# Which engine makes the low parts of the second layer's four key/value weight tiles

## The chip, the core and the metric

The kernel runs on one core of a Trainium2 chip. The metric is the device time of one execution in microseconds (us). The engines are TensorE (PE, matrix products; PEld is its loading of weights), VectorE (DVE), ScalarE (ACT), GpSimd (POOL) and SyncE (SP, which only issues loads here). Each has its own instruction queue and works through it in order; they wait for each other by semaphores.

## The reference, cut to what matters

Two transformer layers run over 512 latent tokens and 256 context tokens of width 1024. Layer 0 is differential attention, layer 1 grouped-query attention with 8 query heads and 2 key/value heads of width 128. What the change touches is the projection to keys and values at the start of layer 1 (`t` is the normalised and modulated stream `h` of the latent tokens, or `hc` of the context):

```python
def project(t):
    p = t @ w_in
    q, k, v, z = jnp.split(p, [GQ_Q_WIDTH, GQ_Q_WIDTH + GQ_KV_WIDTH, GQ_Q_WIDTH + 2 * GQ_KV_WIDTH], axis=-1)
    q = rms_norm(q.reshape(B, L, GQ_HEADS, GQ_HEAD_DIM), qk_g[0])
    k = rms_norm(k.reshape(B, L, GQ_KV_HEADS, GQ_HEAD_DIM), qk_g[1])
```

Keys and values have 256 columns each, for all 768 tokens, and the contraction runs over 1024.

## The kernel before

**Split products.** Every product of the two layers is made of three PE matmuls (`mm3`, L159): each operand is split into a high part, rounded to the matmul's type, and a low part, which is the remainder; high x high, high x low and low x high are summed in PSUM. So each weight tile of 128x1024 passes through `wsplit` (L221): SP loads it into one of two `raw` buffers (L223), ACT writes the high part `whi` (L225), and DVE or POOL writes the low part `wlo` as the difference (L226, by `pieces`, L215). DVE does it in one instruction of 1024 columns, POOL in four of 256:

```python
n = w // -(-w // 256) if eng is nc.gpsimd else w
for i in range(0, w, n):
    eng.tensor_tensor(dst[:, i:i + n], a[:, i:i + n], b[:, i:i + n], op)
```

A raw buffer is free for the next load when both parts are written.

**The stream of tiles.** `WStream` (L237) holds the tiles in the order of their use, and takes the next one as soon as a slot for its two parts is free. Nearly all low parts are DVE's. The exceptions are some of the first tiles of layer 0 and, of the second layer's tiles, those named by `KVE` (L43): tiles 8 to 11 hold the key weights (8 the first half of the contraction, 9 the second) and the value weights (10 and 11 in the same way).

```python
for i in (8, 9, 10, 11):
    ws.add(i, b_w[i], (nc.vector, nc.gpsimd)[KVE[i - 8]])
```

**From layer 0 to layer 1.** The last output product of layer 0 runs over six blocks of 128 tokens (L1365): 0 to 3 are latent, 4 and 5 context. For each block, `resid_a` (L1318) sums squares on ACT (L1292) and multiplies by the gate on DVE (L1322); POOL makes the reciprocal root in two small steps (L421, L422); `resid_b` (L1330) adds the residual on DVE (L1336), ACT sums squares again, POOL adds (L1339, L421), takes the root (L422) and scales the block into `xn` (L1342). Block 5's context rows are loaded by SP into `xn` at L1327. `h1_tr` (L1345) transposes two blocks on PE (L1350), and DVE and ACT make the high and low parts of `h` (L1356 to L1363).

**The key/value stage** follows a written order, `KV` (L44): `k`, `v` are the 24 matmuls of one token block against the key or the value weights (`proj_tok`, L1270: eight contraction steps of three matmuls; steps 0 to 3 read the first tile of the pair, 4 to 7 the second, and each step reads one 256-column piece of it), `t` is one `h1_tr` of the context blocks 4 and 5, and `c` transposes finished keys. The order begins k0, k1, v0, k2, t0, k3. The tiles 8 to 11 are released together at L1458.

**What sets the order of instructions.** The program is written in a certain order, with priorities (`high_priority`, `hot`). A scheduler then simulates it and lets each engine take, each time that it is free, the ready instruction of the highest priority; that order is fixed in the program that runs.

Of the kernel before, what the change touches and what calls it, by code (L numbers as in the profile page):

```python
# [39 lines left out]
PRE = 16.26  # L40
TS = 9.04
HFD = 2
KVE = (0, 1, 0, 1)  # L43
KV = (('k', 0), ('k', 1), ('v', 0), ('k', 2), ('t', 0), ('k', 3), ('c', 0), ('v', 1), ('v', 2), ('t', 1), ('k', 4), ('c', 1), ('c', 2), ('k', 5), ('v', 3), ('v', 4), ('c', 3), ('c', 4), ('v', 5), ('c', 5))  # L44
SPL = 3.06
GAP0 = 6.86
# [41 lines left out]
def tile_backbone(  # L88
# [213 lines left out]
    for i in (8, 9, 10, 11):  # L302
        ws.add(i, b_w[i], (nc.vector, nc.gpsimd)[KVE[i - 8]])
    for kind, i in [("q", 0)] + fill1:
# [1511 lines left out]
```

## Time and profile before

| | us |
|---|---|
| median of three runs | 792.78 (792.57 to 792.84) |
| the profiled execution | 792.77 |
| its span in the profile | 790.8 |
| busy: PE, DVE, ACT, POOL | 776.8, 522.4, 455.4, 324.9 |
| TensorE's granted clock, share of full speed | 0.999 |

The span runs from the first to the last instruction; the 1.97 us between it and the execution's time lie around it. PE is busy for 98% of the span, so an engine that is not PE counts where PE waits for it. The stretch that the change touches is from about 510 to 545 us of the span. In the rows below, an instruction has its start, its length, its engine, its line, its operation, what it writes and reads, and in brackets the idle time of its engine just before it and what ended that. L155 is the line of the helper that issues the matmuls.

### The profile page before, as it was taken

Reading aid. Unit: us, or ns where it says so; the run is one execution under the profiler, and the core shown is the slowest. Engines: PE = TensorE matmul, PEld = TensorE weight load, DVE = VectorE, ACT = ScalarE, POOL = GpSimd, SP = SyncE. Lnnn points to the kernel's source line nnn. Section 1 sums busy time; section 2 is a strip of 40 time slices with the busy share of each in tenths; the row PEclk is TensorE's granted clock in tenths of the full one; section 3 lists DMA queues with packets and bytes.
Section 4 is the critical chain, followed back from the end, with each engine's and each line's share of the span. In section 5 each row is a group of like instructions: output and inputs, shape, how many; then the busy total and the mean of one; then the engine's idle time right before and its main releaser. Section 6 shows DMA issues by size and latency. Waiting matters only on the chain.

```text
span 790.8 us, 14236 instructions
## 1 busy us (share of the span) xinstructions
PE 776.8 (98%) x5446; PEld 699.2 (88%) x5446; DVE 522.4 (66%) x940; ACT 455.4 (58%) x994; POOL 324.9 (41%) x434
## 2 busy tenths in 40 slices
PE   8999999999999999999999999999999999999996
PEld 6688888988887898888979998899999999989986
DVE  4666677786769637866578753567558977565634
ACT  5546546675575644775468843565456676676632
POOL 1121375663338542353425411585446654234101
PEclk9999999999999999999999999999999999999999
DMA  9934211131422322323330151041423512010102
GB/s 339 384 97 148 80 54 59 50 104 67 138 80 83 118 81 68 120 80 107 117 97 31 51 213 54 1 140 53 159 82 101 153 43 81 27 54 28 54 27 107
DMA packets 35092, 77.77 MB, mean 98 GB/s; under 512 B 3408, under 2 KB 10064, under 8 KB 35024
## 3 DMA queue, kind: packets, MB, share of 16 engines
q1 hardware_dynamic: 31168, 71.05, 26.9%
q10 hardware_dynamic: 3856, 5.81, 2.1%
q8 instruction: 43, 0.70, 0.3%
q14 instruction: 25, 0.20, 0.1%
HBM read 70.56 MB, written 2.10 MB: 92 GB/s over the span
## 4 chain that ended last, share of the span: by engine, by line
PE 89%; DVE 3%; ACT 3%; DMA 2%; POOL 1%; issue 1%; SPq 0%; DVEq 0%; ACTq 0%; POOLq 0%
PE bk L155 56%; PE sc L155 10%; PE bk L167 9%; PE sc L994 5%; PE bk L1059 3%; PE bk L1558 3%; PE bk L835 1%; DMA xnt<-in_xlT 1%; PE sc L1023 1%; POOL wlo L219 1%; DMA raw<-in_b_w 1%; DVE al L1063 1%; PE bk L406 1%; PE bk L407 1%; ACT p L1033 0%
## 5 line engine op out<-in xcount | busy, mean ns | idle before, releaser
L155 PE MATMUL bk<-whi,h 128*128 128x256 f32 (+1 forms) x1184 | 243.7, 299 | 0.0
L155 PE MATMUL bk<-h,whi 128*128 128x512 f32 (+2 forms) x864 | 227.9, 347 | 0.0
L155 PEld LDWEIGHTS bk<-whi,h 128*128 128x128 f32 x1184 | 191.8, 191 | 10.5 <-issue 4.0
L155 PE MATMUL bk<-wlo,h 128*128 128x256 f32 (+1 forms) x592 | 175.7, 299 | 0.0
L155 PEld LDWEIGHTS bk<-h,whi 128*128 128x128 f32 x864 | 149.9, 189 | 17.1 <-issue 2.9
L155 PE MATMUL bk<-h,wlo 128*128 128x512 f32 (+2 forms) x432 | 149.6, 346 | 0.0
L233 POOL TENSOR_SCALAR p<-p,sm 128x768 f32<-128x768 f32 (+1 forms) x80 | 71.7, 899 | 163.1 <-DVE sm L1005 63.9
L155 PEld LDWEIGHTS bk<-wlo,h 128*128 128x128 f32 x592 | 112.6, 191 | 3.8 <-issue 0.7
L219 DVE TENSOR_TENSOR wlo<-raw,whi 128x1024 fp32r<-128x1024 f32 (+1 forms) x66 | 80.7, 1226 | 34.4 <-ACT whi L225 34.3
L155 PEld LDWEIGHTS bk<-h,wlo 128*128 128x128 f32 x432 | 81.5, 189 | 7.1 <-issue 0.2
L225 ACT CAST whi<-raw 128x1024 fp32r<-128x1024 f32 x64 | 67.2, 1050 | 32.9 <-PE bk L155 27.8
L1002 ACT ACTIVATE p<-sc,sm 128x768 f32<-128x768 f32 (+1 forms) x68 | 59.5, 878 | 30.6 <-DVE sm L999 30.1
L999 DVE TENSOR_REDUCE sm<-sc 128x1 f32<-128x768 f32 (+1 forms) x68 | 60.3, 917 | 19.2 <-PE sc L994 19.2
L219 POOL TENSOR_TENSOR sz<-sz,za 128x192 f32<-128x192 f32 (+1 forms) x48 | 35.1, 752 | 65.8 <-ACT za L199 65.7
L1010 DVE SCALAR_TENSOR_TENSOR p<-p,sm,p 128x768 f32<-128x768 f32 (+1 forms) x34 | 40.3, 1186 | 7.4 <-POOL p L233 5.1
L994 PE MATMUL sc<-qk,qk 64*128 64x384 f32 (+1 forms) x396 | 43.8, 351 | 0.7 <-ACT p L1002 0.7
L1562 DVE TENSOR_TENSOR al<-bk,ah 128x512 fp32r<-128x512 f32 x48 | 32.1, 686 | 18.4 <-ACT ah L1561 18.2
L1062 ACT CAST ah<-bk 128x512 fp32r<-128x512 f32 x56 | 31.6, 589 | 19.0 <-PE bk L1059 16.6
L1063 DVE TENSOR_TENSOR al<-bk,ah 128x512 fp32r<-128x512 f32 x56 | 37.4, 683 | 6.7 <-ACT ah L1062 6.5
L1543 ACT ACTIVATE p<-sc,sm,qrs 128x768 f32<-128x768 f32 x32 | 31.9, 996 | 15.1 <-DVE sm L1540 8.9
L994 PEld LDWEIGHTS sc<-qk,qk 64*128 64x128 f32 x396 | 32.8, 184 | 7.7 <-issue 3.4
L1561 ACT CAST ah<-bk 128x512 fp32r<-128x512 f32 x48 | 26.9, 588 | 17.9 <-PE bk L1558 14.6
(240 smaller groups left out, 1492.6 us busy)
## 6 DMA issues: line engine op xcount, KB each, us to landing
raw<-in_a_w SPq DMA_DIRECT2D x28, 512.0 KB, 3.5
araw<-in_ada_w SPq DMA_DIRECT2D x12, 1024.0 KB, 5.2
raw<-in_b_w SPq DMA_DIRECT2D x20, 512.0 KB, 3.5
ag<-in_ada SPq DMA_DIRECT2D x16, 512.0 KB, 7.9
raw<-in_w_out SPq DMA_DIRECT2D x16, 512.0 KB, 3.5
sw<-qr ACTq DMA_DIRECT2D x32, 128.0 KB, 2.1
gw<-in_ada_w SPq DMA_DIRECT2D x8, 512.0 KB, 4.1
xnt<-in_xlT SPq DMA_DIRECT2D x4, 512.0 KB, 5.6
```

Source lines behind the costliest of these rows:

```text
L155: i = nc.tensor.matmul(o, a, b, start=start, stop=stop)
L167: nc.tensor.matmul(o, v[:, kt + e, c], a[:, e * 256:e * 256 + 256], start=first and i == 0, stop=last and i == 5)
L219: eng.tensor_tensor(dst[:, i:i + n], a[:, i:i + n], b[:, i:i + n], op)
L225: nc.scalar.copy(hi, r)
L233: (nc.vector if eng == "v" else nc.gpsimd).tensor_scalar(dst, src, s_, 1.0, ALU.mult, ALU.mult)
L994: prev = nc.tensor.matmul(sc[m][:, j if nk == T else m, :w], a[r, tok], b[r, c], start=i == 0, stop=i == 2)
L999: nc.vector.tensor_reduce(mx, scv, AX.XY if nk == T else AX.X, ALU.max, negate=True)
L1002: nc.scalar.activation(pv_, scv, AF.Exp, bias=mx, accum_out=l[:, m:m + 1])
L1010: nc.vector.scalar_tensor_tensor(ps_[0], pt, r, ps_[0], ALU.mult, ALU.add)
L1063: nc.vector.tensor_tensor(al, tr, f32(ah), ALU.subtract)
L1543: nc.scalar.activation(pt.rearrange("p (j n) -> p j n", j=2), scv, AF.Exp, scale=sr, bias=nmx, accum_out=l)
L1562: nc.vector.tensor_tensor(al, tr, f32(ah), ALU.subtract)
```

## The change

The four entries of `KVE` are turned round: POOL makes the low parts of tiles 8 and 10, DVE those of tiles 9 and 11. Before, DVE makes 8 and 10, and POOL 9 and 11. Loads, high parts, products and the written order stay as they are.

```diff
 HFD = 2
-KVE = (0, 1, 0, 1)
+KVE = (1, 0, 1, 0)
```

## Rows read from the trace of the kernel before

**Rows 1.** The page: span, and PE's busy time, share and instructions.

```profile
span 790.8 us, 14236 instructions
...
PE 776.8 (98%) x5446; PEld 699.2 (88%) x5446; DVE 522.4 (66%) x940; ACT 455.4 (58%) x994; POOL 324.9 (41%) x434
```

**Rows 2.** Windows: length, busy PE, PEld, DVE, ACT, POOL, clock, DMA share, GB/s.

```profile
517.00:530.00 13.00, 12.63 (x107) 12.43 (x105) 8.31 (x11) 9.23 (x27) 10.67 (x16) 1.00 0.59 199
530.00:556.00 26.00, 25.65 (x216) 25.65 (x217) 17.10 (x44) 12.80 (x38) 14.08 (x20) 1.00 0.14 42
556.00:576.00 20.00, 20.00 (x170) 20.00 (x169) 10.41 (x25) 8.67 (x30) 10.35 (x18) 1.00 0.45 159
...
700.00:760.00 60.00, 59.56 (x402) 55.19 (x401) 34.39 (x60) 35.66 (x71) 16.21 (x20) 1.00 0.11 36
```

**Rows 3.** Waits of PE, 440 to 791 us: total, times, longest.

```profile
PE sc L1350 <- POOL xn L1342: 0.7, 1, 0.7
PE sc L155 <- ACT p L1543: 0.4, 1, 0.4
```

**Rows 4.** Timeline of PE: the first key matmuls, and around 530 us.

```profile
517.00 0.48 PE L155 MATMUL bk<-whi,h 128*128 128x256 f32 x2
517.32 0.28 PE L155 MATMUL bk<-wlo,h 128*128 128x256 f32 x1
...
529.36 0.28 PE L155 MATMUL bk<-whi,h 128*128 128x256 f32 x1
530.35 1.09 PE L1350 MATMUL sc<-ident,xn 128*128 128x128 f32 x8 [0.72 <-POOL xn L1342]
```

**Rows 5.** Chain that ended last, 500 to 545 us: start, length, what.

```profile
518.49 4.74 DMA raw<-in_b_w
...
523.26 1.06 ACT whi L225
...
527.93 0.49 POOL sm L421
...
529.17 1.13 POOL xn L1342
```

**Rows 6.** Timeline of POOL, 514 to 527 us.

```profile
514.37 0.89 POOL L1339 TENSOR_SCALAR sm<-sm 128x1 f32<-128x1 f32 x1 [2.38 <-ACT jk L1292]
515.34 3.13 POOL L219 TENSOR_TENSOR wlo<-raw,whi 128x256 fp32r<-128x256 f32 x4
518.42 0.34 POOL L421 TENSOR_TENSOR sm<-sm 128x1 f32<-128x1 f32 x2
...
524.39 2.83 POOL L219 TENSOR_TENSOR wlo<-raw,whi 128x256 fp32r<-128x256 f32 x4 [1.98 <-ACT whi L225]
```

**Rows 7.** Timeline of DVE, 512 to 523 us.

```profile
512.03 1.42 DVE L1336 SCALAR_TENSOR_TENSOR gate<-u,sm,gate 128x512 f32<-128x512 f32 x2 [0.53 <-POOL sm L422]
...
513.96 1.22 DVE L219 TENSOR_TENSOR wlo<-raw,whi 128x1024 fp32r<-128x1024 f32 x1
...
521.31 1.63 DVE L1336 SCALAR_TENSOR_TENSOR xn<-u,sm,xn 128x512 f32<-128x512 f32 x1 [0.45 <-POOL sm L422]
```

**Rows 8.** Timeline of ACT, 512 to 526 us.

```profile
512.09 1.06 ACT L225 CAST whi<-raw 128x1024 fp32r<-128x1024 f32 x1
...
514.18 1.04 ACT L225 CAST whi<-raw 128x1024 fp32r<-128x1024 f32 x1
...
525.36 0.18 ACT L1292 ACTIVATION_READ_ACCUMULATOR jk<-xn 128x1 f32 x1
```

**Rows 9.** Timeline of SP's queue of loads, 515 to 517 us.

```profile
515.21 0.33 SPq L223 DMA_DIRECT2D raw<-in_b_w  x1
516.87 0.33 SPq L1327 DMA_DIRECT2D xn<-in_xc  x1
```

**Rows 10.** The page's DMA issues: count, KB each, median us to landing.

```profile
raw<-in_b_w SPq DMA_DIRECT2D x20, 512.0 KB, 3.5
```

**Rows 11.** POOL's line 1339, 440 to 530 us: least, median, greatest ns.

```profile
L1339 POOL TENSOR_SCALAR sm<-sm x6: 213/224/887, 492.5 to 527.3; 128x1 f32<-128x1 f32 x6
```

## The prediction

> **What bounds the kernel now.** I read the page first: TensorE (PE) is busy for 776.8 of 790.8 us [rows 1], so time can only be won or lost where PE idles. The table of windows [rows 2] shows where: from 556 to 576 us it is busy throughout, in 517 to 530 it lacks 0.37 us, in 530 to 556 another 0.35, in 700 to 760 another 0.44. The waits of PE over the whole second layer [rows 3] name only two: 0.7 us for GpSimd's (POOL's) `xn`, and 0.4 us for an exponential, far from the change. PE's timeline gives the first its place [rows 4]: the last matmul before it starts at 529.36, the next work, the eight transposes of normalised row block 5, only at 530.35. Matmuls of 256 columns follow each other at 0.12 us (three in the 0.36 us of one contraction step), so PE was free at 529.48 and starts 0.87 us late; the trace counts 0.72 of it as idle, and I use 0.72.
>
> The chain of waits [rows 5] and POOL's timeline [rows 6] then say why. All four key/value weight tiles pass through here. Tile 11's low part holds POOL from 524.39 to 527.22, ahead of the three small steps and the scaling that make `xn`; that scaling starts at 529.17 and releases PE at 530.35. So one of the two low parts that POOL makes now stands in the chain that PE waits for. It is the fourth tile's, and that one goes to VectorE (DVE).
>
> **The change part by part.** Work in all: DVE makes two low parts at 1.22 us each [rows 7] before and after, POOL two of four pieces at 2.83 and 3.13 us [rows 6]. Nothing is added; cost 0. What moves is which tile waits for which queue.
>
> Tile 11 leaves POOL. POOL's four pieces (2.83 us) no longer stand at 524.39. The sums that L1339 and L421 read come from ScalarE (ACT), whose square sums of block 5 follow tile 11's cast (it ends at 523.26 + 1.06 = 524.32 [rows 5]) by two passes, the second of which is read out by 525.36 + 0.18 = 525.5 [rows 8]. Today L421 starts at 527.93 and `xn` ends at 530.30, 2.37 us later [rows 5]. From 525.5 it would end at about 527.9, 1.6 us before PE is free at 529.48. So the 0.72 goes, and with 1.6 us in hand. DVE takes tile 11 in its place: 1.22 us, beside PE. What is late next is nothing that the waits of PE show until 700 us.
>
> Tile 10 comes to POOL. Its load needs a raw buffer, which is freed now by DVE's tile 8 at 515.18 (the issue is at 515.21 [rows 9]). After the change the first of the two buffers is free when DVE has made tile 9 or POOL tile 8, both at about 516.3 to 516.5 (next paragraphs): 1.2 us later. A load takes 3.5 us in the median and the slowest here 4.74 [rows 5, 10], the cast 1.06, the four pieces 2.83 to 3.13. So tile 10's low part is done between 516.4 + 3.5 + 1.06 + 2.83 = 523.8 and 516.4 + 4.74 + 1.06 + 3.13 = 525.3. That is early enough for POOL to start on `xn` at 525.5. PE comes to the first value product at 517.00 + 2 x 8 x 0.36 = 522.8 and wants the pieces from 522.9 on: between nothing and 1.3 us of waiting. I take 0, by the row that it is nearest to: tile 11's low part is late today by far more (due at 522.8 + 4 x 0.36 = 524.2, complete at 527.22) and PE has no idle before 529.5 [rows 2, 4, 6], since the order that the scheduler writes puts the third key product and transposes in between. 1.3 stays as the upper end.
>
> SP's queue: tile 10's load moves back from 515.21 to about 516.4, next to the context rows' load at 516.87 [rows 9], which is also on block 5's path; tile 11's load, at 518.49 now [rows 5], can go at about 517. Three loads of 512 KB then start within 0.7 us rather than 3.3. If each takes as long as the slowest of today, the context rows land 0.6 us later (516.87 + 4.74 = 521.6, against the DVE step that uses them at 521.31 [rows 7]). That is inside the 1.6 us in hand; cost 0, upper end 0.6 off the same cover.
>
> Tile 8 comes to POOL. Its cast starts at 512.09 and takes 1.06 [rows 8], so its input is there at 513.15. POOL is idle for 2.38 us before 514.37, waiting for ACT [rows 6]. The four pieces can run from 513.2 to 516.3 (3.13 us, the longer of the two sets); PE first reads a low part at 517.32 [rows 4] and one more piece every 0.36 us. Cost 0, with 1 us in hand. Behind the pieces stands L1339 of block 4, now at 514.37 and then at about 516.4; but its followers L421 come only at 518.42 today, behind tile 9's pieces [rows 6], and those pieces are gone, so block 4 is no later. The other end of this cost is 2.4 us; it is the second rival.
>
> Tile 9 goes to DVE. The cast ends at 514.18 + 1.04 = 515.2 [rows 8], DVE lost tile 8's 1.22 us at 513.96, so the part is ready by about 516.5; PE wants it at 517.32 + 4 x 0.36 = 518.8. POOL makes it by 518.47 today. Cost 0, and more in hand than now.
>
> **Sum.** The profiled execution took 792.77 us (span 790.8 and 1.97 around it), and the median of the runs is 792.78, so the two stand for each other. 792.77 - 0.72 = 792.05; I say **792.1 us**, a gain of 0.09%. About 0.2% (1.6 us) is what a measurement of this kernel can tell from no change, so this counts as the same.
>
> **Where rows speak against it.** DVE's instructions with two inputs in on-chip memory hold POOL up: L1339 on POOL takes 224 ns in the median of six and 887 once [rows 11], that once from 514.37 to 515.26, and DVE's tile 8 ends at 515.18 [rows 6, 7]. It goes the other way too: DVE's step at 521.31 took 1.63 us where the two steps of the block before took 1.42 together [rows 7]. The Trainium skill ("GPSIMD Engine Reference", section Key points) says that GpSimd shares its SBUF interfaces with VectorE and contends with instructions of two SBUF inputs; the trace agrees. The same page (section Engine selection) would give element-wise work to VectorE, GpSimd being about twice as slow with two inputs; here it is 3.13 against 1.22, and by that rule the tile that PE needs first should not go to POOL. What this would do is worked out in the second rival.
>
> **Rivals.**
> 1. *The wait stays.* Block 5 is held by something other than tile 11: its context rows land late because three loads now run together, or tile 10's pieces sit in front of L1339. For it: tile 10's worst case ends at 525.3, the loads' at 521.6, and if both slip by another microsecond or two the 1.6 in hand are gone. Against: that needs two worst cases at once. Time: 792.8, within 0.4. Chance 0.24.
> 2. *PE waits for tile 8's low part at 517.3: slower.* If the order puts POOL's L1339 first, as it stands now, the pieces run from 515.34 for 3.13 us to 518.47; DVE's tile 9 (1.22 us from about 515.8) now falls into that stretch and holds them up to 519.7. PE wants the first piece at 517.32. If it waits for the whole tile it stands for 2.4 us; the 0.72 at 530 is still won, so 792.77 + 2.4 - 0.7 = **794.5** (+0.2%). If PE waits piece by piece, the first is there at some 517.3 and next to nothing is lost. It decides from the moment that the last piece ends later than 517.32 + 0.72 = 518.0. For it: the hold-up is in the trace. Against: POOL's idle stretch lies open before 514.37, and where tile 9's and tile 11's casts came just ahead of ACT's sums, the order put all four pieces ahead of the small steps [rows 6]. Chance 0.15, half of it beyond +0.2%.
> 3. *The order downstream changes.* The order on every engine comes from a simulated schedule, and one that runs from 517 us on differently may fall out differently to the end. To gain, there is only the idle of 0.37 + 0.35 + 0.44 = 1.16 us up to 760 [rows 2], so 791.6 at best, and perhaps half a microsecond of stalls that modelled ends of matmuls hide: 791.1. To lose, there is more room: two more waits like the one at 530 make 793.5, five of them 795.6. Against: PE is so full from 543 to 576 that the order should settle again. Chance 0.13: 0.05 faster, 0.06 slower, the rest between.
>
> That the swap does not happen is no case: the engine is named in the call, and nothing else decides it.
>
> **How the numbers follow.** Forecast 0.48 (791.6 to 792.5), rivals 0.24, 0.15 and 0.13. Beyond 0.2% slower than 792.78, over 794.4: half of rival 2 and half of rival 3, 0.14 in all. Beyond 0.2% faster, under 791.2: 0.05, from rival 3 alone. The rest, 0.81, is the same. The range from 791.1 to 794.5 holds forecast, rival 1, the bound of rival 2 and the gain of rival 3; it leaves out mainly the long losses of rival 3 and mishaps that come together.
>
> **What would show it.** In the changed kernel's trace: POOL makes low parts from about 513.2 and again between 521 and 525, none after; DVE makes one near 515.5 and one near 525; L1339 to `xn` of block 5 ends near 528; PE's wait for `xn` is gone from its list and the 517 to 530 window is full. Wrong, if PE waits for a low part at 517 or 523, if its wait for `xn` is still there, or if the windows after 543 differ by more than a few tenths of a microsecond; then the order downstream has changed and the cause lies there.

## The result and the profile after

The changed kernel takes **794.88 us** in the median of ten runs (794.22 to 797.15), the kernel before, beside it on the same chip, 792.69 (792.39 to 793.29). The ratio is 1.0029, with a 95% interval from 1.0021 to 1.0038: 2.2 us slower, just outside the range that was given, and on the other side of no change. The changed kernel's profiled execution took 797.15 us (span 795.2), the longest of its ten; the others lie between 794.22 and 795.64. So its trace holds some 2 us that a usual run does not have. An estimate below puts 1.7 of them on TensorE's clock; there is no trace of a usual run, so the sizes are taken from timed experiments.

The page of the changed kernel, the lines that answer to [rows 1]:

```profile
span 795.2 us, 14236 instructions
...
PE 778.6 (98%) x5446; PEld 699.9 (88%) x5446; DVE 526.5 (66%) x940; ACT 456.0 (57%) x994; POOL 324.7 (41%) x434
```

Its table of windows, columns as in [rows 2]:

```profile
517.00:530.00 13.00, 12.71 (x105) 12.24 (x104) 9.73 (x13) 9.21 (x24) 10.18 (x15) 1.00 0.54 182
530.00:543.00 13.00, 10.79 (x77) 10.31 (x76) 9.14 (x28) 5.50 (x19) 6.81 (x12) 0.87 0.09 32
543.00:556.00 13.00, 13.00 (x112) 13.00 (x110) 8.83 (x15) 5.93 (x17) 6.87 (x8) 1.00 0.20 60
556.00:576.00 20.00, 20.00 (x170) 20.00 (x169) 10.27 (x22) 9.13 (x29) 6.84 (x13) 1.00 0.42 147
```

The instructions are the same in number. The loss is in one window: from 530 to 543 us PE lacks 2.21 us (before, 0.35 from 530 to 556) and issues 77 matmuls, where the full window behind it has 112. A further part is the clock: the granted share is 0.87 there, and 0.57 from 534 to 538, so PE ran for a while at the lower of its two levels (1.2 instead of 2.4 GHz), right behind its longest wait. An estimate of what that cost, from the row: (1 - 0.87) x 13 = 1.7 us. PE's timeline marks the stage: from the first key product to the first transpose of queries it is 56.24 us before (517.00 to 573.24) and 60.29 after (517.35 to 577.64); from there to the last matmul it is 211.25 in both. Nothing changes behind the key/value stage.

The waits of PE from 440 to 796 us of the changed kernel, as [rows 3]:

```profile
PE bk L155 <- DVE kn L1430: 1.6, 1, 1.6
PE sc L1350 <- POOL xn L1342: 0.6, 1, 0.6
PE sc L155 <- ACT p L1543: 0.4, 1, 0.4
PE bk L155 <- POOL wlo L219: 0.2, 1, 0.2
```

PE's timeline at the two long ones, as [rows 4]:

```profile
531.38 1.09 PE L1350 MATMUL sc<-ident,xn 128*128 128x128 f32 x8 [0.60 <-POOL xn L1342]
534.09 0.55 PE L155 MATMUL bk<-whi,h 128*128 128x256 f32 x1 [1.61 <-DVE kn L1430]
```

The chain that ended last, from 500 to 550 us, as [rows 5]:

```profile
518.80 4.46 DMA raw<-in_b_w
...
523.29 1.06 ACT whi L225
...
525.57 2.37 DVE xn L1336 x2
...
527.97 5.33 DMA gq<-in_b_qk_g
...
533.42 0.62 DVE kn L1430 x2
```

The wait for `xn` that the change was to remove (0.7 in [rows 3]) is still there with 0.6, and a longer one stands behind it: for the normalised keys `kn`, whose gains `gq` (L1383) are loaded late. (The bracket of `kn` in DVE's rows below names POOL's L1410; the chain has the load of `gq`, which landed at 533.30, and where that load comes early, in gq_early below, the wait for `kn` is 0.2.) The chain names the way there, and three timelines show its links. SP's queue of loads, as [rows 9]:

```profile
518.37 0.80 SPq L223 DMA_DIRECT2D raw<-in_b_w  x2
519.23 0.42 SPq L1327 DMA_DIRECT2D xn<-in_xc  x1
```

POOL, as [rows 6]:

```profile
513.57 4.78 POOL L219 TENSOR_TENSOR wlo<-raw,whi 128x256 fp32r<-128x256 f32 x4 [1.24 <-ACT whi L225]
518.43 0.22 POOL L1339 TENSOR_SCALAR sm<-sm 128x1 f32<-128x1 f32 x1
...
523.12 4.25 POOL L219 TENSOR_TENSOR wlo<-raw,whi 128x256 fp32r<-128x256 f32 x4 [1.34 <-ACT whi L225]
527.63 0.38 POOL L1339 TENSOR_SCALAR sm<-sm 128x1 f32<-128x1 f32 x1 [0.25 <-ACT jk L1292]
...
530.20 1.12 POOL L1342 TENSOR_SCALAR xn<-xn,sm 128x1024 f32<-128x1024 f32 x1
```

DVE, as [rows 7]:

```profile
513.70 2.38 DVE L1363 TENSOR_TENSOR h<-hf,h 128x512 fp32r<-128x512 f32 x2
515.99 1.76 DVE L219 TENSOR_TENSOR wlo<-raw,whi 128x1024 fp32r<-128x1024 f32 x1
...
524.37 1.27 DVE L219 TENSOR_TENSOR wlo<-raw,whi 128x1024 fp32r<-128x1024 f32 x1 [1.29 <-ACT whi L225]
525.57 2.36 DVE L1336 SCALAR_TENSOR_TENSOR xn<-u,sm,xn 128x512 f32<-128x512 f32 x2
527.85 1.28 DVE L1363 TENSOR_TENSOR h<-hf,h 128x512 fp32r<-128x512 f32 x2
533.42 0.61 DVE L1430 SCALAR_TENSOR_TENSOR kn<-bk,qrs,gq 128x128 f32<-128x128 f32 x2 [4.29 <-POOL qrs L1410]
```

POOL's low part of tile 8 takes 4.78 us, not 3.13, with DVE's L1363 and tile 9 beside it, which are slowed too (2.38 against 1.28 for the same pair at 527.85; 1.76 against 1.27). It ends at 518.35, and SP's load of tile 10, which takes over its buffer, is issued at 518.37; before it was 515.21 [rows 9]. The order on SP's queue has changed as well: both value tiles stand ahead of the context rows, which go from 516.87 to 519.23. Three loads now start within 0.9 us. What came early before is late on every queue behind it. The context rows land at 524.60, 3.6 us later than before (521.02). Tile 11's low part stands on DVE ahead of block 5's residual (L1336), which starts at 525.57 instead of 521.31 [rows 7]. Where a residual waits for nothing but its rows, it starts 0.1 us behind their landing (dve_all below), so of these 4.3 us tile 11 holds some 0.9, and the late rows the rest. POOL's pieces of tile 10 stand ahead of L1339 (523.12 to 527.37), but L1339 then waits another 0.25 us for ACT, so they are not what holds it. ACT's queue issues `gq` only at 527.97, behind block 5's square sums (before: 523.65), to land 5.33 us later.

### The profile page after: what moved, and what is told of

Same layout as the page of the kernel before. It is cut to its first block, busy times and chain, and to the rows that moved or that the text cites. A ratio compares the mean times of both kernels' runs of the same rounds, so it can differ in the third digit from the quotient of the medians.

```text
span 795.2 us, 14236 instructions
## 1 busy us (share of the span) xinstructions
PE 778.6 (98%) x5446; PEld 699.9 (88%) x5446; DVE 526.5 (66%) x940; ACT 456.0 (57%) x994; POOL 324.7 (41%) x434
## 4 chain that ended last, share of the span: by engine, by line
PE 87%; DVE 4%; ACT 3%; DMA 3%; issue 1%; POOL 1%; SPq 0%; DVEq 0%; ACTq 0%
PE bk L155 55%; PE sc L155 10%; PE bk L167 8%; PE sc L994 5%; PE bk L1558 3%; PE bk L1059 2%; PE bk L835 1%; DMA xnt<-in_xlT 1%; DMA sw<-qr 1%; DMA gq<-in_b_qk_g 1%; ACT whi L225 1%; DVE al L1063 1%; DMA raw<-in_b_w 1%; PE sc L1023 1%; POOL wlo L219 1%
## 5 line engine op out<-in xcount | busy, mean ns | idle before, releaser
L1062 ACT CAST ah<-bk 128x512 fp32r<-128x512 f32 x56 | 31.6, 589 | 19.0 <-PE bk L1059 16.6
L1059 PE MATMUL bk<-ident,p 128*128 128x128 f32 x224 | 35.2, 276 | 2.0 <-DVE gate L1133 1.1
```

Source lines behind the costliest of these rows:

```text
L1059: nc.tensor.transpose(tr[:, e * 256 + i * P:e * 256 + (i + 1) * P], a[:, j * P:(j + 1) * P], ident)
```

## The experiments

In the table "over before" is the ratio with its 95% interval, against runs of the kernel before on the same chip; an interval reaches 0.7 to 1.0 us to either side. "Stage" is the time on PE's timeline of the one profiled execution from the first key product to the first transpose of queries.

| run | median us | over before | stage us |
|---|---|---|---|
| before | 792.5 to 792.8 | | 56.24 |
| after | 794.88 | 1.0029 [1.0021, 1.0038] | 60.29 |
| after_again | 794.83 | 1.0027 [1.0017, 1.0038] | 60.24 |
| keys_only | 794.40 | 1.0021 [1.0012, 1.0030] | 57.85 |
| values_only | 795.31 | 1.0029 [1.0017, 1.0040] | 58.67 |
| gq_early | 794.11 | 1.0019 [1.0010, 1.0028] | 57.40 |
| after_late11 | 793.47 | 1.0012 [1.0004, 1.0021] | 56.80 |
| gq_late11 | 793.26 | 1.0008 [0.9999, 1.0016] | 56.61 |
| gq_xc | 795.59 | 1.0037 [1.0025, 1.0050] | 58.80 |
| gq_xc_late11 | 794.98 | 1.0029 [1.0017, 1.0041] | 58.37 |
| after_own | 798.32 | 1.0073 [1.0060, 1.0085] | 61.84 |
| own_ordered | 794.13 | 1.0020 [1.0011, 1.0029] | 57.64 |
| before_own | 793.94 | 1.0018 [1.0009, 1.0027] | 58.10 |
| before_xn_first | 794.27 | 1.0021 [1.0012, 1.0030] | 57.70 |
| pool_9_only | 793.25 | 1.0007 [0.9998, 1.0016] | 56.86 |
| dve_all | 793.46 | 1.0011 [1.0003, 1.0020] | 57.84 |

**after_again: the changed kernel once more.** No edit.

> The changed kernel once more, unaltered, because the execution that was profiled (797.15 us) is the slowest of its ten (median 794.88). Theory A (block 5 is late: SP's queue has the loads of tiles 10 and 11, held up by POOL's tile 8, ahead of block 5's context rows; from there PE waits for the key norm's gains gq, whose load stands on ACT's queue behind block 5's square sum, and for xn): median 794.2 to 795.6, and the two waits of PE are there again at about 530 to 534 us, the one behind gq shorter than 1.6 us or without the drop of the granted clock after it. Theory B (the order further down has changed, and the waits at 530 are chance): the two waits are much smaller, and PE loses its time after 543 us.

794.83 us, and the same trace: waits of 1.5 us for `kn` and 0.6 for `xn`. Its profiled execution (796.69) is again the longest, so the two profiles are the two longest of 17 runs. The slowdown is real; the 1.5 to 1.6 us at `kn`, and the clock of 0.87 from 530 to 543 us in both, are what these two executions show.

**keys_only and values_only: half of the change each.**

keys_only:

```diff
-KVE = (1, 0, 1, 0)
+KVE = (1, 0, 0, 1)
```

> Half of the change: POOL makes the low part of tile 8 and DVE that of tile 9; tiles 10 (DVE) and 11 (POOL) as in the kernel before. SP's order has tiles 10 and 11 ahead of block 5's context rows, as in the changed kernel. Theory A, by which tile 8 on POOL and SP's order are the cause: 794.2 to 795.6, as slow as the whole change. A rival, by which the value tiles are the cause (tile 10's four pieces on POOL, tile 11 on DVE ahead of block 5's residual): 792.2 to 793.2.

values_only:

```diff
-KVE = (1, 0, 1, 0)
+KVE = (0, 1, 1, 0)
```

> The other half: POOL makes the low part of tile 10 and DVE that of tile 11; tiles 8 (DVE) and 9 (POOL) as before. SP's order has block 5's context rows between the two loads, as in the kernel before. Theory A: no loss, and the gain that the prediction saw in tile 11's leaving POOL: 791.9 to 792.7, PE's wait for xn gone. The rival, by which the value tiles are the cause: 794 to 795.5.

keys_only, with POOL on tiles 8 and 11, costs most of the loss by itself and meets its first expectation: again 4.78 us for tile 8, again both value loads ahead of the context rows (518.02 and 518.87), and PE waits 1.1 us for `xn`. POOL's pieces of tile 11 take 4.16 us there, with block 5's later residual beside them, and hold L1339 until 528.30 (before: 2.83 us, until 527.22). values_only keeps the loads as before and does take the wait for `xn` away, as the prediction's step said; but it is no faster, as PE waits elsewhere: 0.54 us for `kn` at 531.59, 0.31 at 556.57 and 0.92 for `vl` at 558.29. Its first expectation was wrong. Its time lies in the rival's range, but not for the reason given there: tile 11 stands behind block 5's residual on DVE (525.60; the residual runs from 521.53 to 523.43). The wait for `vl` comes behind the low part of a later weight tile (on DVE from 556.69 to 557.90), so the order has changed further down the stage. A loss as large as the whole change's thus comes here with the loads on time and the residual first. The halves don't add up: 1.6 and 2.6 us alone, 2.1 together.

**gq_early, after_late11, gq_late11: the two late placements undone, one by one and together.** gq_early issues the gains' load early on ACT's queue, into a buffer that is free then; after_late11 has DVE make tile 11's low part behind block 5's residual; gq_late11 does both.

```diff
-    xn = {}
+    xn, early = {}, last_of(nc.scalar)
...
-        gq = t1p.tile([P, 2, P], F32, name="gq")
-        nc.scalar.dma_start(gq, b_qk_g.partition_broadcast(P))
+        gq = con.tile([P, 2, P], F32, name="gq")
+        with tc.issue_after(early): nc.scalar.dma_start(gq, b_qk_g.partition_broadcast(P))
```

```diff
...
-        pieces(eng, lo, r, f32(hi), ALU.subtract)
+        with tc.issue_after(mark[0]) if key == 11 else nullcontext(): pieces(eng, lo, r, f32(hi), ALU.subtract)
...
-    ws.release(*wout_keys(0, c, n))
+    mark.append(last_of(nc.vector)); ws.release(*wout_keys(0, c, n))
```

> The changed kernel with one load moved: the key norm's gains gq get memory of their own and are loaded before layer 0's last product ends, so that nothing waits for them; the order on PE, DVE, POOL and SP stays as it is, and on ACT only this load moves. Theory A: PE's wait behind gq (1.6 us in the profile, with some 1.7 us at the lower clock after it) goes, xn's 0.6 stays: 792.8 to 793.6, that is 1.3 to 2.1 us under the changed kernel. Theory B: no change, 794.5 to 795.3.

> gq_early with DVE's low part of tile 11 put behind block 5's residual; SP's order stays. Theory A1: the residual waits for its rows, which land at 524.4, so it starts 0.7 earlier than in gq_early and the time falls by 0.3 to 0.7 at most, 793.4 to 793.8. Theory A2: 0.7 to 1.0 less, 793.1 to 793.4, with PE's wait for xn gone.

> The changed kernel with one order undone: DVE's low part of tile 11 is issued behind block 5's residual instead of ahead of it; the key-norm gains' load stays where it is, on ACT's queue behind block 5's square sums. Theory A (that one placement is the head of the later waits: residual, square sum, gains' load and key norm all stand behind it): the residual starts near 524.0 instead of 525.6, the gains' load is issued near 526.4 and has landed by 531.7, PE's waits for xn and kn are 0.5 or less each; 793.0 to 793.7. Theory B (it takes both edits, the gains' load is a loss of its own): the wait for kn stays at 1 us or more, 794.0 to 795.0.

Over the kernel before on its own chip, the changed kernel stands at +2.07 us (after_again), gq_early at +1.35, after_late11 at +0.95, gq_late11 at +0.62. So the gains' load is worth 0.7 alone, outside both expectations and between them, and tile 11's place on DVE 1.1; together they give back 1.45 of the 2.07, less than their sum. The trace of after_late11 fits that: with the residual earlier, `gq` goes out at 526.55 by itself. These are rough sizes. The single runs of gq_early and the changed kernel overlap; nine of after_late11's eleven runs stand less over their before than any of the changed kernel's 17, and it meets its first expectation in time, in the residual's start and in both waits. In gq_early and in after_late11 the granted clock is full again throughout the window in which it had fallen; gq_early's row:

```profile
530.00:543.00 13.00, 12.19 (x102) 11.72 (x101) 11.35 (x31) 6.40 (x20) 9.13 (x13) 1.00 0.02 6
```

What is left of PE's waits in after_late11 is tile 11 itself, which that expectation did not have:

```profile
PE bk L155 <- DVE wlo L219: 0.7, 1, 0.7
PE sc L155 <- ACT p L1543: 0.4, 1, 0.4
PE bk L155 <- DVE kn L1430: 0.2, 1, 0.2
```

No wait for `xn` is left. Its DVE timeline has the residual ahead of tile 11 and 1.4 us earlier than in the changed kernel, 0.1 us behind the landing of its rows (524.06):

```profile
524.16 2.35 DVE L1336 SCALAR_TENSOR_TENSOR xn<-u,sm,xn 128x512 f32<-128x512 f32 x2 [1.53 <-POOL wlo L219]
526.43 1.21 DVE L219 TENSOR_TENSOR wlo<-raw,whi 128x1024 fp32r<-128x1024 f32 x1
```

DVE makes the tile in one instruction, so no piece of it is there before 527.64, and PE waits until 527.70; on POOL, before, the first of four pieces was done at 525.13. So on DVE tile 11 costs in either place: ahead of the residual by what stands behind it, behind the residual by itself.

**gq_xc and gq_xc_late11: the context rows on another queue.** Both have gq_early's edit; block 5's rows are loaded from ACT's queue, so that they need not stand behind the value tiles on SP's; the second has the late tile 11 too.

```diff
-            nc.sync.dma_start(t, xc[(m - NQ) * P:(m - NQ + 1) * P, :])
+            (nc.sync if m == NQ else nc.scalar).dma_start(t, xc[(m - NQ) * P:(m - NQ + 1) * P, :])
```

> gq_early (794.11 us) with block 5's context rows loaded from ACT's queue instead of SP's, so that they no longer stand behind the loads of tiles 10 and 11; DVE and POOL keep their order. Theory A1 (SP's queue is what makes block 5 late): DVE's residual of block 5 starts near 522 instead of 525.1, PE's 0.6 for xn and 0.2 for the key norm go: 793.0 to 793.4. Theory A2 (DVE's own order is what holds it: tile 11's low part, which waits for its late load, stands ahead of the residual): the residual still starts when tile 11 is done, about 525, and the time stays within 0.2 of 794.1.

> gq_early with both: the context rows from ACT's queue and tile 11's low part behind the residual. Either theory: the residual starts near 522, POOL's pieces of tile 10 are what is left ahead of xn, PE's waits for xn and the key norm go, and only the wait for tile 10's pieces (0.8 us in gq_early) is left: 792.8 to 793.3. If it stays at 794, block 5 is held by POOL's tile 10 and not by SP or DVE.

Both missed in time, and both are slower than their twins without this edit, by 1.6 and 1.7 us (each over its own before). The rows go out at 517.0. In gq_xc the residual still starts behind tile 11 on DVE, as theory A2 has it, but at 526.69, since tile 11 is later too. In gq_xc_late11 it starts at 522.73, and L1339 then stands behind tile 10's pieces on POOL until 528.88. But now tile 10's load starts 1.1 us behind a load already under way, and its high part begins at 523.08 and 523.53 instead of 521.55 (after_late11): PE waits 0.6 and 1.1 us for `whi` and 0.8 and 0.7 for tile 10's pieces. Loads of 512 KB that are under way together land one behind the other: at 521.98, 523.26 and 524.60 in the changed kernel, at 520.58, 523.05 and 524.44 in gq_xc. Putting one first made another the late one, so these runs have no early rows without a late tile 10.

**after_own, own_ordered, before_own: the loads of tiles 10 and 11 don't wait for POOL.** Tiles 10 and 11 get two buffers of their own. own_ordered also sets two orders by hand: tile 10's pieces behind block 4's scaling, tile 11's low part behind block 5's residual.

```diff
-        r = wp.tile([P, 1024], F32, tag="raw", name=nm("raw"), bufs=2)
+        r = (rawp[0] if key in (10, 11) else wp).tile([P, 1024], F32, tag="raw", name=nm("raw"), bufs=2)
...
-    u0, ss = {}, {}
+    u0, ss = {}, {}; rawp.append(bp)
```

> The changed kernel, but the loads of tiles 10 and 11 get two buffers of their own, so neither waits until POOL has written tile 8's low part. Theory A (the loss comes from that wait: tile 8's low part, held up to 4.8 us beside DVE's instructions, frees its buffer only at 518.3, and three loads then start together): the two loads are issued well before 517, tile 8's low part still takes over 4 us on POOL, POOL's scaling of block 5 no longer has tile 10's pieces in front of it, PE's wait for xn falls under 0.2 and those for kn and low parts go; from the first key product to the first query transpose 56.4 us or less (60.2 in the changed kernel, 56.2 before), time 791.9 to 793.0. Rival B (the loss is the sharing of POOL and DVE itself, or the order of the stage, not the buffer): at least 58 us for the stage and 794.0 to 795.5.

> The kernel before with the same two buffers for tiles 10 and 11. Its tile 10 already loads from 515.2 on; tile 11, now from 518.5 on, can come earlier. Theory A (what PE waits for at 530 is tile 11's low part in POOL's queue, as its load comes late): xn is done before PE asks for it, that wait (0.7 us) goes and the time is 791.9 to 792.4. Rival B (the order changes and gives it back elsewhere, as with values_only and pool_9_only): 792.6 to 794.0.

> The changed kernel with buffers of their own for tiles 10 and 11 (as in after_own) and two orders set by hand: POOL makes tile 10's low part behind block 4's scaling, DVE tile 11's behind block 5's residual. Theory A (what after_own lost comes from the order that the scheduler wrote, not from the early loads): stage of 56.8 us or less, 792.3 to 793.4, no wait of PE over 1 us. Rival B (two low parts on POOL with DVE's instructions beside them are too slow for the stage wherever they stand): tile 10's pieces again take over 4 us, PE waits 1 us or more for h, kn or xn, 794.5 to 798.

Here a theory fell: that the time comes back when tiles 10 and 11 are loaded early. They are (from 462.66 and 463.67 on in after_own), and after_own is the slowest of all. But the runs do not take the whole delay away. The weight tiles behind them in SP's order now wait for the buffers of tiles 8 and 9, and block 5's context rows still stand behind these two loads (after_own):

```profile
518.00 0.80 SPq L223 DMA_DIRECT2D raw<-in_b_w  x2
518.90 0.38 SPq L1327 DMA_DIRECT2D xn<-in_xc  x1
```

The rows land at 524.13, and in own_ordered at 523.89, about as late as in after_late11 (524.06). So what the late rows cost is not measured by these runs. The timeline of POOL in after_own has tile 8 unchanged and tile 10 early, as meant:

```profile
513.17 4.81 POOL L219 TENSOR_TENSOR wlo<-raw,whi 128x256 fp32r<-128x256 f32 x4 [1.23 <-ACT whi L225]
...
519.17 4.43 POOL L219 TENSOR_TENSOR wlo<-raw,whi 128x256 fp32r<-128x256 f32 x4
523.59 1.12 POOL L1342 TENSOR_SCALAR gate<-gate,sm 128x1024 f32<-128x1024 f32 x1
```

But that tile 10 now stands ahead of block 4's scaling, 3.9 us later than in the changed kernel (519.71), and the order of the stage behind it differs: PE waits 2.4 us for an `h` at 542.56, and the granted clock is 0.89 from 543 to 556. The time lies beyond both expectations. own_ordered, with the loads still early, wins 4.2 of the 5.8 us back, yet ends at 794.13: its tile 10 (520.15 to 523.85 on POOL) stands ahead of block 5's first reciprocal root, so the residual starts at 524.68, no earlier than in after_late11. Its time is between both expectations. Early loads of tiles 10 and 11 alone bring nothing here; early rows with them were not tried. before_own (+1.4 us) missed its first expectation and lies in its rival's range: PE's wait for `xn` falls to 0.4, and one of 0.7 for `kn` comes in.

**before_xn_first, pool_9_only, dve_all: the gain that was predicted, tried in other ways.** before_xn_first leaves every tile on its engine and has POOL make tile 11's pieces behind block 5's scaling; pool_9_only and dve_all give POOL only tile 9, or none. before_xn_first:

```diff
-        pieces(eng, lo, r, f32(hi), ALU.subtract)
+        with tc.issue_after(mark[key]) if key in mark else nullcontext(): pieces(eng, lo, r, f32(hi), ALU.subtract)
...
-    ws.release(*wout_keys(0, c, n))
+    mark[11] = last_of(nc.gpsimd); ws.release(*wout_keys(0, c, n))
```

> The kernel before, with POOL's low part of tile 11 issued behind block 5's scaling instead of ahead of it. Theory A (the step of the prediction called Tile 11 leaves POOL, without moving any tile to another engine): xn ends near 527.9 instead of 530.3, PE's wait for it goes, 791.9 to 792.4. Rival B (PE then comes to tile 11's low part before POOL has made it, about 531): a wait for wlo of 0.5 to 2 us takes its place, 793 to 794.5.

pool_9_only:

```diff
-KVE = (0, 1, 0, 1)
+KVE = (0, 1, 0, 0)
```

> POOL makes only tile 9's low part, DVE those of 8, 10 and 11: the one step of the prediction that was to bring the gain (tile 11 leaves POOL), without tiles 8 and 10 coming to it. If that step was right by itself: PE's wait for xn gone, nothing else late, 791.9 to 792.5. Rival: DVE with three tiles is late with the residual or with the key norm, and PE waits there: 793 to 795.

dve_all:

```diff
-KVE = (0, 1, 0, 1)
+KVE = (0, 0, 0, 0)
```

> DVE makes all four low parts, POOL none; raw buffers as before. Theory A (low parts on POOL are what holds buffers and xn up; DVE makes one in 1.2 us and has room): loads of tiles 10 and 11 are issued by 517, no xn wait, 791.9 to 793.0. Rival B (DVE becomes the engine that the stage waits for: two more low parts of 1.2 us stand in front of block 5's residual and of the high-low splits that PE waits for): xn goes but PE waits for h, kn or vl by 1 us or more, 793.5 to 795.5.

All three missed their first expectation; the times of before_xn_first and pool_9_only lie in their rivals' ranges, though PE waits for other things than the rivals named, and dve_all lies just under its rival's. In before_xn_first POOL's timeline shows `xn` and what now follows it:

```profile
526.46 1.12 POOL L1342 TENSOR_SCALAR xn<-xn,sm 128x1024 f32<-128x1024 f32 x1
527.55 3.69 POOL L219 TENSOR_TENSOR wlo<-raw,whi 128x256 fp32r<-128x256 f32 x4
531.20 0.70 POOL L1411 TENSOR_TENSOR qrs<-qrs,mhalf 128x2 f32<-128x2 f32 x1
```

PE's timeline shows who waits:

```profile
527.64 1.09 PE L1350 MATMUL sc<-ident,xn 128*128 128x128 f32 x8 [0.27 <-POOL xn L1342]
532.60 0.39 PE L155 MATMUL bk<-whi,h 128*128 128x256 f32 x1 [0.80 <-DVE kn L1430]
```

`xn` is done at 527.6, 2.7 us earlier than before, and PE takes it earlier; but the pieces now stand ahead of the keys' root (L1411), and PE waits 0.80 us for `kn`: 794.27. pool_9_only has `xn` at 528.3 and a new wait of 0.8 for `h` at 543.80, 793.25. On DVE's timeline of dve_all the low parts and the residual run at full speed, with no low part on POOL beside them:

```profile
514.33 1.22 DVE L219 TENSOR_TENSOR wlo<-raw,whi 128x1024 fp32r<-128x1024 f32 x1
516.07 1.22 DVE L219 TENSOR_TENSOR wlo<-raw,whi 128x1024 fp32r<-128x1024 f32 x1
...
523.07 1.42 DVE L1336 SCALAR_TENSOR_TENSOR xn<-u,sm,xn 128x512 f32<-128x512 f32 x2 [1.69 <-DMA xn<-in_xc]
```

But its context rows, whose load has tile 11's 0.4 us behind it, land at 523, and PE waits 0.8 for `xn` and 0.8 for `h`: 793.46, 0.9 us over before. None of the variants is faster than the kernel before; the best two, at +0.6 us, can't be told from it: their intervals include 1.

## Why the prediction was wrong

**Tile 11 leaves POOL.** This is the step that failed, on both of its sides. The cost side was one sentence, "DVE takes tile 11 in its place: 1.22 us, beside PE", at no price. It asked what the 1.22 us cost and not what is queued behind them on DVE. That is block 5's residual, the start of the very chain to `xn` that was to be shortened, and DVE can begin tile 11 only at 524.37, when its high part is there. after_late11, which turns round this one order, is 1.1 us better, and PE then waits 0.7 us for tile 11 itself. The gain side was right in its mechanism: where tile 11 alone leaves POOL (pool_9_only), `xn` ends 2 us earlier and its wait falls from 0.72 to 0.27. But it rested on "What is late next is nothing that the waits of PE show until 700 us", and a list of waits shows only what came last, not how close the next thing was. In pool_9_only PE then waits 0.8 us for `h`; before_xn_first, which moves no tile, loses the gain 5 us later at `kn`. No order that was tried kept the 0.72 us; whether one could is not shown.

From the forecast to the result it is 2.8 us, in rough sizes 0.7 that was not gained, 1.1 from tile 11's place, and 0.95 that after_late11 still stands over before. In that last part the next two steps lie, not separated.

**Tile 8 comes to POOL.** Sized at 3.13 us and cost 0; measured 4.78, to 518.35. The hold-up by DVE was read from the trace (0.887 us against 0.224 for L1339 [rows 11]) but used only for the second rival, not for this sum. PE itself didn't wait at 517.3: it reads the first low piece at 517.55, piece by piece, so that rival's wait did not come. That its price, 794.5, lies near the result is chance.

**SP's queue and tile 10.** Both steps took tile 10's load to be freed by whichever of tiles 8 and 9 was done first, at 516.4. Its buffer is tile 8's, and it went out at 518.37; POOL's pieces were done at 527.37 instead of 523.8 to 525.3. The context rows, taken as at most 0.6 us late (521.6 against their landing at 521.02; against the 521.31 that the prediction names it is 0.3), were issued 2.4 us later and behind both tiles, since the order on SP's queue was written anew, and landed 3.6 us later. That alone is more than the 1.6 us in hand. The trace shows that these loads are late, not what that costs: the own-buffer runs left the rows late, and gq_xc made tile 10 late in their place.

**The key-norm gains.** No step named them, because their load was on time before (issued 523.65). They stand on ACT's queue behind block 5's square sums, and went 4.3 us back with them; alone they are worth some 0.7 us.

**The rivals.** The first, that the wait stays, described what is in the trace: three loads together, tile 10's pieces ahead of L1339, `xn` at 531.3. Its price stopped there, at 792.8; the same lateness went on into tile 11's place on DVE and into the gains. The third, a change downstream, did not happen behind the stage: 211.2 us from the first transposed query to the last matmul in all runs. The half microsecond of hidden stalls in its lower bound is shown by no run.

**What stays open.** What the late rows and the slow tile 8 cost by themselves was not measured, and values_only shows that a loss of the same size can come without either. gq_late11's last 0.6 us over before is within its interval. Why POOL's tile 8 moved ahead of L1339 and the loads ahead of the context rows is the scheduler's doing; its reasons stay open.

## What to carry to other kernels

When work moves to another engine, price it by what stands behind it in that engine's queue, and by when its input comes: a late input at the head of an in-order queue delays everything behind it, however short the work is. Where a stage is full and its order comes from a scheduler, removing one visible wait of 0.7 us is not a gain of 0.7 us: look for the second-latest thing before counting it. Take the duration of a POOL instruction from a row in which DVE is as busy as it will be after the change.

## What the runs showed of the hardware

The hold-up between POOL and DVE goes both ways, and is larger than the rows before had it. Four POOL pieces of 128x256 with two inputs took 2.83 us [rows 6] at best and 4.81 at worst; a pair of L1363 on DVE took 1.28 without them and 2.38 beside them, a low part 1.22 and 1.76, the residual's pair 1.41 and 2.36. In the changed kernel tile 8's pieces, L1363 and tile 9 took 513.57 to 518.35 together; one after the other they would be 2.83 + 1.28 + 1.22 = 5.33 us, so side by side they saved 0.55. The Trainium skill ("GPSIMD Engine Reference", section Key points) states this contention, and the trace agrees. The same page of the Trainium skill, section Engine selection, would give all four low parts to VectorE: in dve_all each took 1.22 us, but the kernel was 0.9 us slower than with two of them on POOL.

Behind waits of 0.6 and 1.6 us, which began 1.7 us apart, PE's granted clock was lower: 0.87 of full speed in the 13 us around them (0.87 again behind 0.6 and 1.5 in after_again), and 1.00 in the same window where the second wait was 0.2 (gq_early) or where 1.1 and 0.2 followed each other (keys_only). after_own has the same behind its wait of 2.4 us, with 0.89. So a wait on PE can cost more than its own length: an estimate from the row of 0.87 is 1.7 us on top of the waits.
